# A gated product split whole instead of in four blocks, and three scalings queued behind the gate's splits, in a two-layer decoder trunk

## The chip, the cores and the metric

The kernel runs on one core of one Trainium2 chip. The metric is device time of one execution in microseconds (us), the median of several executions. Engine names are those of the profile: PE (matrix multiply), PEld (its weight loads), DVE (vector), ACT (activation), POOL (GpSimd), SP (the queue that issues most DMAs).

## What is computed

The input is one sequence of 1024 positions by 1024 channels. Layer 0 mixes positions with a chunked gating MLP, layer 1 with dilated attention, and each mixer is followed by a dense MLP. The change touches only the mixer of layer 0:

```python
def _chunk_gating_mixer(h, w_in, ln_g, ln_b, w_s, b_s, w_out):
    uv = gelu(h @ w_in)
    u, v = split(uv, 2, axis=-1)
    v = layer_norm(v, ln_g, ln_b)
    # chunks of 128 positions, 8 channel groups, causal 128x128 mixer w
    mixed = einsum('gts,bnsgc->bntgc', w, v) + b_s
    return (u * mixed) @ w_out
```

## The kernel before

Products are made of 32-bit operands split in two: `split` (L222 to L224) writes `hi`, a rounded copy, on ACT (L223) and `lo`, the rest, on DVE (L224). A product then takes three matmuls a step: weight hi with both halves of the data, weight lo with the data's hi. A weight tile needs two loads of 128x512, two copies on ACT and two subtractions on DVE.

The order of PE's instructions is the order of the text; for all other engines a list scheduler decides at build time, by priority and by when it thinks that operands are there. Once built, each engine runs its instructions in order, so one that waits holds up all behind it. `tc.issue_after(x)` puts the instructions of its block behind x on x's engine.

The work around the change, in order of time in the profile:

- **v** (up to about 130 us). x arrives in 16 tiles of 128x512 (`load_x`); `scaled(s, k)` makes the split tile `y` for half s of the positions and channel tile k (L647 on ACT, L648 on DVE) and a square of the tile for the norm (L276 on ACT, summed on POOL at L281 or on DVE at L285). In the first of three groups of chunks (`gi == 0`) the loop over k also splits the weights `w_v[k]`. At k == 7 it adds `gate_weights()` to the side work and calls `scaled(1, 0..2)` for the second half. `gate_weights` splits the causal mixer's weights into `wsh` and `wsl` (L669 to L673), multiplies them by ones and folds the sums into `rb` (L681). Then come the norm's root (L253), the activation of v (L729) and, for each of 8 chunks, layer norm, split and mixing (`spatial`).
- **u** (about 130 to 213 us). 16 tiles of 128x512, one for each channel tile m and half s, 24 matmuls each, in three PSUM banks `mm` in turn. The order is m = 0, 1, 2 for both halves, then 3, then 4, then 5, 6, 7, in each case half 0 before half 1. `u_out` empties a bank: scaling by the norm (L784, DVE, high priority; it sets the bank free), Gelu (L785, ACT), and four products of 128x128 with the mixed v (L788, DVE), written into the four `vg` tiles of the half. `u_split(s)`, called after the last tile of half s, splits the products for the next matmul in 8 tiles x 4 blocks of 128x128: 32 copies on ACT and 32 subtractions on DVE.
- **w_o** (from about 214 us). Tiles in the same three banks; `add_h` (L336, DVE) empties them. The first tile reads all of half 0's split products.
- **Side work beside u and w_o**: `prepare` makes weights for the attention ahead of time. For each of six units it loads four tiles (`t<-in_w_qkv`, by SP), forms sums and differences on DVE (L527, L528, L533, L536), splits seven of them (tiles `tr`) and writes each split back by two DMAs (`wd<-tr`, L524). The four loads of the next unit are issued by SP in turn with those writes; L527 is the first that needs them (the second and third).

Of the kernel before, what the change touches and what calls it, by code (L numbers as in the profile page):

```python
# [12 lines left out]
F32 = mybir.dt.float32  # L13
F32R = mybir.dt.float32r
AF = mybir.ActivationFunctionType
ALU = mybir.AluOpType
# [15 lines left out]
def half(s):  # L32
    return slice(s * HALF, (s + 1) * HALF)


def blk(b, n=1):
    return slice(b * P, (b + n) * P)
# [89 lines left out]
def trunk(ctx: ExitStack, tc: tile.TileContext, xT, w_u, w_v, w_o, w_s, b_s, w_qkv, w_vt, w_bo, rel,  # L127
          w_up, w_dn, w_dl, vecs, onehot, outT):
    nc = tc.nc
    flow = Flow()  # L130
# [11 lines left out]
    def temp():  # L142
        return tpool.tile([P, HALF], F32, tag="t", name="t")
# [4 lines left out]
    def rtemp():  # L148
        return tpool.tile([P, HALF], F32R, tag="t", name="tr")

    def slot(shape=(P, S), dtype=F32, name="s"):

        return slots.tile(list(shape), dtype, tag="s", name=name)

    class Pair:
# [14 lines left out]
    def pair(name="y"):  # L170
        return Pair(slot((P, 2, HALF), F32R, name))
# [19 lines left out]
    def at_bank():  # L191
        return psa.tile([P, HALF], F32, tag="at", name="at")
# [27 lines left out]
        nc.tensor.matmul(idle[:, 0:P], ones, ones, start=True, stop=True)  # L220

    def split(hi, lo, src, engine=None):  # L222
        nc.scalar.activation(hi, src, AF.Copy)  # L223
        (engine or nc.vector).tensor_tensor(lo, src, hi.bitcast(F32), op=ALU.subtract)  # L224

    def weight(src, own=None):
        lo = wpool.tile([P, D], F32R, tag="w", name="wlo")
# [398 lines left out]
    vg = {}  # L626
    wsh = slot((P, 8, P), F32R, "wsh")
    wsl = slot((P, 8, P), F32R, "wsl")
# [11 lines left out]
    def scaled(s, k):  # L640

        x, g = h[k][:, half(s)], vec[:, 0, k:k + 1]
        hi, lo = pair().both()
        if (s, k) == (0, 0):
            nc.vector.tensor_scalar(hi, x, g, None, op0=ALU.mult)
        else:
            begun.append(nc.scalar.activation(hi, x, AF.Copy, scale=g).ins)  # L647
        nc.vector.scalar_tensor_tensor(lo, x, g, hi.bitcast(F32), op0=ALU.mult, op1=ALU.subtract)  # L648
        ys[s].append((hi, lo))
        sq[s].add(k)  # L650
# [3 lines left out]
        nc.scalar.activation(rsb[:, half(s)], pb, AF.Copy)  # L654
        yield 0

    gate_raw = []

    def gate_loads():
        for i in range(2):  # L660
# [5 lines left out]
    def gate_weights():  # L666

        one = rtemp()[:, 0:P]
        nc.scalar.activation(one, ones, AF.Copy)  # L669
        for i, w3 in enumerate(gate_raw):  # L670
            nc.gpsimd.affine_select(w3, w3, pattern=[[0, 4], [1, P]], compare_op=ALU.is_ge, fill=0.0,
                                    base=0, channel_multiplier=-1)
            split(wsh[:, 4 * i:4 * i + 4, :], wsl[:, 4 * i:4 * i + 4, :], w3)  # L673
        yield 6000
        for i in range(2):
            ps = at_bank()
            for e, w in enumerate((wsh, wsl)):
# [55 lines left out]
    for gi, chunks in enumerate(((0, 1, 2), (3, 4, 5), (6, 7))):  # L733
        banks = {}
        for k in range(KT):
            if gi == 0:
                load_x(0, k)
                if k >= 5:
                    load_x(1, k - 5)
            if gi == 0:  # L740
                scaled(0, k)

            with tc.issue_after(roots[0] if k == 1 else gelus[5]) if gi == 1 and k else nullcontext():
                w = weight(w_v[k])
            if gi == 0:
                if k == 5:
                    with tc.issue_after(begun[1]):
                        gate_loads()
                if k == 7:
                    flow.add(gate_weights())  # L750
                    for i in range(3):
                        scaled(1, i)
            if gi == 1:
                if k == 0:
                    flow.add(spatial())
                if k < 5:
                    load_x(1, k + 3)
                    scaled(1, k + 3)
            if k == 0:
                for i, n in enumerate(chunks):  # L760
                    for f in range(2):
                        banks[n, f] = mm_bank() if 2 * i + f >= 6 - MMB else at_bank()
            order = [(e, i, n, f) for i, n in enumerate(chunks) for f in range(2) for e in range(3)]
            if gi == 0 and k == 0:
                order.sort(key=lambda t: (t[0], t[3]))
            for e, i, n, f in order:
                x, c = ys[n // 4][k], blk(n % 4)
                matmul(banks[n, f], x[e == 1][:, c], w[e == 2][:, half(f)], start=(k == 0 and e == 0),
                       stop=(k == 7 and e == 2))
                if e == 2:  # L770
                    flow.pump()
                if k == 7 and e == 2 and f == 1:
                    if i == 0 and gi < 2:
                        for _ in sq[gi].sums():
                            pass
                        sq[gi].rms(rs[:, 4 * gi:4 * gi + 4])
                        flow.add(spread_rms(gi), 4000)
                    else:
                        v_out(banks, chunks[:i + 1])

    def u_out(m, s, ps):
        t = temp()
        with tc.high_priority(offset=PRIO):
            nc.vector.tensor_tensor(t, ps, rsb[:, half(s)], op=ALU.mult)  # L784
        nc.scalar.activation(t, t, AF.Gelu)  # L785
        for b in range(4):
            x = vg[4 * s + b][:, blk(m)]
            nc.vector.tensor_tensor(x, x, t[:, blk(b)], op=ALU.mult)  # L788

    def u_split(s):  # L790
        out = []
        for m in range(8):
            hi, lo = pair().both()
            for b in range(4):
                split(hi[:, blk(b)], lo[:, blk(b)], vg[4 * s + b][:, blk(m)])
            out.append((hi, lo))
        return out

    us = []
    for tiles in ((0, 1, 2), (3,), (4,), (5, 6, 7)):  # L800
        w = [weight(w_u[m]) for m in tiles]
        if tiles[0] == 3:
            flow.add(prepare(PREPARED[0], PACE[0]))
        for s in range(2):
            for i, m in enumerate(tiles):
                b = mm_bank()
                mm(b, w[i], KCOLS, ys[s])
                flow.until(lambda: gated[4 * s + 3].t is not None)
                u_out(m, s, b)
            if tiles[-1] == 7:  # L810
                us.append(u_split(s))


    sq = [Square(half(0)), Square(half(1))]
# [814 lines left out]
    whole = {}  # L1629
# [316 lines left out]
```

## Time and profile before

| | us |
|---|---|
| median of 3 runs | 2121.05 (2119.27 to 2121.4) |
| profiled execution | 2123.05 |
| its span on the core | 2121.3 |
| PE busy | 2096.6 (99%) |
| DVE busy | 1580.1 (74%) |
| ACT busy | 1183.2 (56%) |
| POOL busy | 497.2 (23%) |

The profiled execution took 2123.05 us, of which 2121.3 us are the span that the profile shows; 1.75 us lie around it. PE is busy almost throughout, so time can be lost or won only where PE pauses. The views that matter are the list of what PE waited for, the time line of the engine that it waited for there, and the granted clock in stretches.

### The profile page before, as it was taken

Reading aid. Unit: us, or ns where it says so; the run is one execution under the profiler, and the core shown is the slowest. Engines: PE = TensorE matmul, PEld = TensorE weight load, DVE = VectorE, ACT = ScalarE, POOL = GpSimd, SP = SyncE. Lnnn points to the kernel's source line nnn. Section 1 sums busy time; section 2 is a strip of 40 time slices with the busy share of each in tenths; the row PEclk is TensorE's granted clock in tenths of the full one; section 3 lists DMA queues with packets and bytes.
Section 4 is the critical chain, followed back from the end, with each engine's and each line's share of the span. In section 5 each row is a group of like instructions: output and inputs, shape, how many; then the busy total and the mean of one; then the engine's idle time right before and its main releaser. Section 6 shows DMA issues by size and latency. Waiting matters only on the chain.

```text
span 2121.3 us, 30732 instructions
## 1 busy us (share of the span) xinstructions
PE 2096.6 (99%) x10160; PEld 1734.1 (82%) x10160; DVE 1580.1 (74%) x2902; ACT 1183.2 (56%) x2387; POOL 497.2 (23%) x368
## 2 busy tenths in 40 slices
PE   9999999999999999999999999999999999999998
PEld 7888788888888888778888888888888888888887
DVE  7877859766689998888746666766985446987776
ACT  7645536566665555345556665766555556544432
POOL 2000114333223233430000000002442232433244
PEclk9999999999999999999999999999999999999999
DMA  6328913678765767643865656582256443655432
GB/s 219 117 86 287 320 45 121 206 271 271 258 222 192 233 215 224 229 163 147 309 205 149 183 157 175 166 279 70 75 199 204 159 150 128 205 164 160 143 114 80
DMA packets 224756, 387.10 MB, mean 182 GB/s; under 512 B 39897, under 2 KB 67668, under 8 KB 224596
## 3 DMA queue, kind: packets, MB, share of 16 engines
q1 hardware_dynamic: 215456, 383.77, 55.0%
q10 hardware_dynamic: 9140, 1.36, 0.4%
q8 instruction: 80, 1.31, 0.3%
q14 instruction: 80, 0.66, 0.1%
HBM read 252.24 MB, written 132.81 MB: 182 GB/s over the span
## 4 chain that ended last, share of the span: by engine, by line
PE 89%; DVE 5%; DMA 2%; ACT 1%; issue 1%; POOL 1%; SPq 0%; DVEq 0%; POOLq 0%; ACTq 0%
PE mm L195 46%; PE at L195 41%; PE at L202 2%; DMA h<-in_xT 1%; DVE y L224 1%; DVE t L224 1%; DVE wp L224 0%; DVE r L441 0%; DMA r<-in_w_vt 0%; DVE hx L224 0%; DVE b L446 0%; DMA r<-in_w_dn 0%; DVE t L1867 0%; DVE h L336 0%; DVE h L1074 0%
## 5 line engine op out<-in xcount | busy, mean ns | idle before, releaser
L224 DVE TENSOR_TENSOR wp<-r,wp 128x512 fp32r<-128x512 f32 (+3 forms) x399 | 325.0, 820 | 123.0 <-ACT wp L223 120.7
L223 ACT ACTIVATE wp<-r 128x512 fp32r<-128x512 f32 (+3 forms) x399 | 235.9, 596 | 314.1 <-PE at L195 194.7
L195 PE MATMUL mm<-t,wp 128*128 128x512 f32 x1368 | 345.2, 396 | 0.6 <-DVE t L996 0.6
L195 PE MATMUL at<-hx,wp 128*128 128x512 f32 x1452 | 341.1, 389 | 1.7 <-DVE h L1074 1.7
L195 PEld LDWEIGHTS at<-hx,wp 128*128 128x128 f32 x1452 | 272.1, 188 | 60.0 <-DVE h L1074 3.3
L195 PEld LDWEIGHTS mm<-t,wp 128*128 128x128 f32 x1368 | 250.6, 188 | 53.4 <-DVE t L996 1.0
L281 POOL TENSOR_TENSOR t<-t 128x512 f32<-128x512 f32 (+1 forms) x60 | 77.4, 1291 | 814.3 <-ACT t L276 647.3
L195 PE MATMUL at<-y,wp 128*128 128x512 f32 x1008 | 245.3, 389 | 0.0
L195 PE MATMUL mm<-hx,wp 128*128 128x512 f32 x984 | 234.2, 389 | 0.7 <-ACT mm L1097 0.7
L195 PEld LDWEIGHTS at<-y,wp 128*128 128x128 f32 x1008 | 189.0, 188 | 39.6 <-issue 0.4
L195 PEld LDWEIGHTS mm<-hx,wp 128*128 128x128 f32 x984 | 184.6, 188 | 39.4 <-ACT mm L1097 1.1
L195 PE MATMUL mm<-y,wp 128*128 128x512 f32 x816 | 210.2, 397 | 1.1 <-DVE y L224 0.6
L379 POOL TENSOR_TENSOR t<-r 128x512 f32<-128x512 f32 (+3 forms) x62 | 83.2, 1342 | 478.3 <-DMA r<-in_w_up 142.2
L195 PEld LDWEIGHTS mm<-y,wp 128*128 128x128 f32 x816 | 149.1, 188 | 33.0 <-DVE y L224 1.0
L224 DVE TENSOR_TENSOR hx<-t,hx 128x512 fp32r<-128x512 f32 x192 | 159.8, 837 | 5.8 <-ACT hx L223 5.7
L195 PE MATMUL mm<-y,whi 128*128 128x512 f32 x512 | 158.4, 390 | 2.0 <-DVE t L784 2.0
L223 ACT ACTIVATE hx<-t 128x512 fp32r<-128x512 f32 x192 | 118.7, 627 | 24.5 <-DMA t<-hid 16.0
L195 PE MATMUL at<-t,wp 128*128 128x512 f32 x552 | 130.6, 389 | 0.0
L381 POOL TENSOR_TENSOR r<-r 128x512 f32<-128x512 f32 (+3 forms) x62 | 90.8, 1465 | 165.8 <-DVE wp L224 148.6
L195 PEld LDWEIGHTS at<-t,wp 128*128 128x128 f32 x552 | 103.6, 188 | 21.5
L1074 DVE TENSOR_TENSOR h<-h,at 128x512 f32<-128x512 f32 x144 | 97.8, 680 | 27.3 <-PE at L195 26.8
L195 PEld LDWEIGHTS mm<-y,whi 128*128 128x128 f32 x512 | 95.5, 188 | 21.9 <-issue 2.4
(247 smaller groups left out, 3498.3 us busy)
## 6 DMA issues: line engine op xcount, KB each, us to landing
t<-hid SPq DMA_DIRECT2D x182, 256.0 KB, 4.1
wd<-tr SPq DMA_DIRECT2D x154, 256.0 KB, 3.2
wp<-wd SPq DMA_DIRECT2D x77, 512.0 KB, 4.2
hid<-t SPq DMA_DIRECT2D x140, 256.0 KB, 2.9
r<-in_w_up SPq DMA_DIRECT2D x120, 256.0 KB, 2.9
r<-in_w_dn SPq DMA_DIRECT2D x80, 256.0 KB, 2.7
hid<-b SPq DMA_DIRECT2D x56, 256.0 KB, 2.8
r<-in_w_v SPq DMA_DIRECT2D x48, 256.0 KB, 3.1
```

The lines of the kernel that those rows point to most:

```text
L195: nc.tensor.matmul(out, lhsT, rhs, **kw)
L202: nc.tensor.transpose(out, src, ident)
L223: nc.scalar.activation(hi, src, AF.Copy)
L224: (engine or nc.vector).tensor_tensor(lo, src, hi.bitcast(F32), op=ALU.subtract)
L281: nc.gpsimd.tensor_tensor(self.acc, self.acc, sq, op=ALU.add)
L379: tt(r3, r[0, 0], r[1, 0], op=ALU.subtract)
L381: tt(r[1, 1], r[1, 0], r[0, 0], op=ALU.subtract)
L1074: return engine.tensor_tensor(hs[i, s], hs[i, s], src, op=ALU.add).ins
```

## The change

In `u_out` 11 of the 16 tiles (all 8 of half 0, and m = 5, 6, 7 of half 1) write the four products into u's own tile `t` instead of into `vg`, and split it at once as one tile of 128x512. The other five (m = 0 to 4 of half 1) are made as before and split in blocks, now right after m = 7 of half 0 instead of at the end of half 1. In the first group of v the side work `gate_weights` is begun before the three scalings, and these stand behind the last gate split on both ACT and DVE.

```diff
     def split(hi, lo, src, engine=None):
-        nc.scalar.activation(hi, src, AF.Copy)
-        (engine or nc.vector).tensor_tensor(lo, src, hi.bitcast(F32), op=ALU.subtract)
+        return (nc.scalar.activation(hi, src, AF.Copy).ins,
+                (engine or nc.vector).tensor_tensor(lo, src, hi.bitcast(F32), op=ALU.subtract).ins)
...
-            split(wsh[:, 4 * i:4 * i + 4, :], wsl[:, 4 * i:4 * i + 4, :], w3)
+            gate_split[:] = split(wsh[:, 4 * i:4 * i + 4, :], wsl[:, 4 * i:4 * i + 4, :], w3)
...
                 if k == 7:
-                    flow.add(gate_weights())
-                    for i in range(3):
-                        scaled(1, i)
+                    gate = gate_weights()
+                    flow.add(gate, next(gate))
+                    with tc.issue_after(gate_split[0]), tc.issue_after(gate_split[1]):
+                        for i in range(3):
+                            scaled(1, i)
...
-    def u_out(m, s, ps):
+    us = [[None] * 8 for _ in range(2)]
+
+    def u_out(m, s, ps, whole):
         t = temp()
         with tc.high_priority(offset=PRIO):
             nc.vector.tensor_tensor(t, ps, rsb[:, half(s)], op=ALU.mult)
         nc.scalar.activation(t, t, AF.Gelu)
         for b in range(4):
             x = vg[4 * s + b][:, blk(m)]
-            nc.vector.tensor_tensor(x, x, t[:, blk(b)], op=ALU.mult)
-
-    def u_split(s):
-        out = []
-        for m in range(8):
-            hi, lo = pair().both()
-            for b in range(4):
-                split(hi[:, blk(b)], lo[:, blk(b)], vg[4 * s + b][:, blk(m)])
-            out.append((hi, lo))
-        return out
+            nc.vector.tensor_tensor(t[:, blk(b)] if whole else x, x, t[:, blk(b)], op=ALU.mult)
+        if whole:
+            x = pair().split(t)
+            us[s][m] = x.hi, x.lo
+
+    def u_split(s, m):
+        hi, lo = pair().both()
+        for b in range(4):
+            split(hi[:, blk(b)], lo[:, blk(b)], vg[4 * s + b][:, blk(m)])
+        us[s][m] = hi, lo
...
-                u_out(m, s, b)
-            if tiles[-1] == 7:
-                us.append(u_split(s))
+                u_out(m, s, b, s == 0 or tiles[-1] == 7)
+            if tiles[-1] == 7 and s == 0:
+                for m in range(tiles[0]):
+                    u_split(1, m)
```

Because a scheduler orders ACT, DVE and SP, three places show what became of this. On PE the instructions are the same ones; only the four products with the gate's weights and a transpose stand a few places earlier. Tile names: `y` is a split tile for a matmul, `t` a temporary, `tr` a split of the side work, `wlo` the rest of a weight, `vg` the gated v. In the changed kernel L784 is L788 and L788 is L792.

ACT at the end of the first group of v, before:

```order
L276 ACTIVATE t<-h 128x512
L647 ACTIVATE y<-h,vec 128x512
L276 ACTIVATE t<-h 128x512
L669 ACTIVATE tr<-ones 128x128
L223 ACTIVATE wsh<-b 128x512 x2
L223 ACTIVATE whi<-r 128x512 x2
L276 ACTIVATE t<-h 128x512
L253 ACT_TABLE_LOAD
```

and now:

```order
L276 ACTIVATE t<-h 128x512
L669 ACTIVATE tr<-ones 128x128
L223 ACTIVATE wsh<-b 128x512 x2
L647 ACTIVATE y<-h,vec 128x512
L276 ACTIVATE t<-h 128x512
L647 ACTIVATE y<-h,vec 128x512
L276 ACTIVATE t<-h 128x512
L647 ACTIVATE y<-h,vec 128x512
L276 ACTIVATE t<-h 128x512
L223 ACTIVATE whi<-r 128x512 x2
L276 ACTIVATE t<-h 128x512
L253 ACT_TABLE_LOAD
```

The copies of the gate's weights moved ahead of the three scalings and their squares; everything from `whi` on stands where it stood, behind the same instructions.

DVE from the scaling of u's tile m = 7, half 0, to that of m = 5, half 1, before:

```order
L784 TENSOR_TENSOR t<-mm,rsb 128x512
L536 TENSOR_TENSOR t<-t 128x512
L224 TENSOR_TENSOR y<-vg,y 128x128
L788 TENSOR_TENSOR vg<-vg,t 128x128 x4
L224 TENSOR_TENSOR y<-vg,y 128x128 x12
L224 TENSOR_TENSOR tr<-t,tr 128x512
L224 TENSOR_TENSOR y<-vg,y 128x128 x2
L224 TENSOR_TENSOR tr<-t,tr 128x512
L224 TENSOR_TENSOR y<-vg,y 128x128 x18
L224 TENSOR_TENSOR wlo<-r,whi 128x512 x2
L224 TENSOR_TENSOR tr<-t,tr 128x512
L784 TENSOR_TENSOR t<-mm,rsb 128x512
```

and now:

```order
L788 TENSOR_TENSOR t<-mm,rsb 128x512
L533 TENSOR_TENSOR t<-t 128x512
L536 TENSOR_TENSOR t<-t 128x512
L792 TENSOR_TENSOR t<-vg,t 128x128 x4
L224 TENSOR_TENSOR tr<-t,tr 128x512
L224 TENSOR_TENSOR wlo<-r,whi 128x512
L224 TENSOR_TENSOR y<-t,y 128x512
L224 TENSOR_TENSOR y<-vg,y 128x128 x20
L224 TENSOR_TENSOR tr<-t,tr 128x512
L224 TENSOR_TENSOR wlo<-r,whi 128x512 x3
L224 TENSOR_TENSOR tr<-t,tr 128x512
L788 TENSOR_TENSOR t<-mm,rsb 128x512
```

Of 33 block splits 20 are left between the two scalings, the five tiles of half 1 that are still made in blocks; one whole split, two splits of weights and one combination of the side work came in. The last `tr` but one (`tr` of unit 3, number 3) stood ahead of 18 of the block splits and stands now behind all 20.

DVE from that scaling (m = 5, half 1) to the next one (m = 6), before:

```order
L784 TENSOR_TENSOR t<-mm,rsb 128x512
L224 TENSOR_TENSOR tr<-t,tr 128x512
L527 TENSOR_TENSOR t<-t 128x512
L788 TENSOR_TENSOR vg<-vg,t 128x128 x4
L528 TENSOR_TENSOR t<-t 128x512
L224 TENSOR_TENSOR y<-vg,y 128x128 x4
L224 TENSOR_TENSOR tr<-t,tr 128x512
L784 TENSOR_TENSOR t<-mm,rsb 128x512
```

and now:

```order
L788 TENSOR_TENSOR t<-mm,rsb 128x512
L527 TENSOR_TENSOR t<-t 128x512
L224 TENSOR_TENSOR tr<-t,tr 128x512
L792 TENSOR_TENSOR t<-vg,t 128x128 x4
L528 TENSOR_TENSOR t<-t 128x512
L224 TENSOR_TENSOR wlo<-r,whi 128x512
L224 TENSOR_TENSOR y<-t,y 128x512
L224 TENSOR_TENSOR tr<-t,tr 128x512
L788 TENSOR_TENSOR t<-mm,rsb 128x512
```

L527, the first to need the next unit's loads, moved from second to first place behind the scaling, and a split of weights came in.

SP where the loads of the next unit stand, before:

```order
L524 DMA wd_7_149<-tr 128x512
L184 DMA r<-in_w_o 128x512
L524 DMA wd_7_149<-tr 128x512
L524 DMA wd_3_152<-tr 128x512 x2
L184 DMA t<-in_w_qkv 128x512 x4
L524 DMA wd_4_153<-tr 128x512 x2
```

and now:

```order
L524 DMA wd_7_149<-tr 128x512 x2
L184 DMA r<-in_w_o 128x512
L524 DMA wd_3_152<-tr 128x512
L184 DMA t<-in_w_qkv 128x512
L524 DMA wd_3_152<-tr 128x512
L184 DMA t<-in_w_qkv 128x512 x3
L524 DMA wd_4_153<-tr 128x512 x2
```

Three of the four loads still stand behind the write of that `tr`, number 3 (`wd_3`); one load went ahead of it.

More of the change, by code (lines that the diff above doesn't have):

```diff
@@ L655, in spread_rms @@
         yield 0
-    gate_raw = []
+    gate_raw, gate_split = [], []
     def gate_loads():
@@ L787, in u_out @@
             x = vg[4 * s + b][:, blk(m)]
-            nc.vector.tensor_tensor(x, x, t[:, blk(b)], op=ALU.mult)
-    def u_split(s):
-        out = []
-        for m in range(8):
-            hi, lo = pair().both()
-            for b in range(4):
-                split(hi[:, blk(b)], lo[:, blk(b)], vg[4 * s + b][:, blk(m)])
-            out.append((hi, lo))
-        return out
-    us = []
+            nc.vector.tensor_tensor(t[:, blk(b)] if whole else x, x, t[:, blk(b)], op=ALU.mult)
[7 more added lines that the diff above has]
+        us[s][m] = hi, lo
     for tiles in ((0, 1, 2), (3,), (4,), (5, 6, 7)):
```

## The prediction

> **What bounds the kernel now.** First the page: PE is busy 99% of the span.
>
> ```profile
> PE 2096.6 (99%) x10160; PEld 1734.1 (82%) x10160; DVE 1580.1 (74%) x2902; ACT 1183.2 (56%) x2387; POOL 497.2 (23%) x368
> ```
>
> The change takes no instruction from PE. So it can gain only what PE waits in the stages of v, u and w_o, and lose only by a new wait. The list of what PE waited for, asked for the first 100 us and for 100 to 345 us, holds three waits worth the name (line, releaser, us in total, times, longest):
>
> ```profile
> PE at L195 <- DVE wlo L224: 2.3, 1, 2.3
> PE at L195 <- ACT vg L729: 1.0, 1, 1.0
> PE mm L195 <- DVE t L784: 2.0, 1, 2.0
> ```
>
> PE's time line places them (start, duration, what, idle before it):
>
> ```profile
> 43.19 0.50 PE L195 MATMUL at<-wlo,y 128*128 128x512 f32 x1 [2.28 <-DVE wlo L224]
> 45.79 1.22 PE L195 MATMUL at<-whi,y 128*128 128x512 f32 x2 [0.97 <-ACT vg L729]
> 215.89 0.70 PE L195 MATMUL mm<-y,whi 128*128 128x512 f32 x2 [1.98 <-DVE t L784]
> ```
>
> Two pauses stand at the end of the first group of v, one at the first tile of w_o. Between and after them, up to 345 us, PE streams, and all that ACT and DVE do there is hidden. The chain of waits gives PE's pace: 213 matmuls in 48.41 us, 0.227 us each, so a tile of 24 takes 5.45 us.
>
> ```profile
> 148.53 48.41 PE mm L195 x213
> ```
>
> **The change, part by part.**
>
> *Whole splits.* DVE's time line around the third pause:
>
> ```profile
> 203.32 0.69 DVE L784 TENSOR_TENSOR t<-mm,rsb 128x512 f32<-128x512 f32 x1
> 205.58 2.51 DVE L224 TENSOR_TENSOR y<-vg,y 128x128 fp32r<-128x128 f32 x12
> 209.01 0.69 DVE L224 TENSOR_TENSOR tr<-t,tr 128x512 fp32r<-128x512 f32 x1
> 209.61 3.73 DVE L224 TENSOR_TENSOR y<-vg,y 128x128 fp32r<-128x128 f32 x18
> 213.24 1.31 DVE L224 TENSOR_TENSOR wlo<-r,whi 128x512 fp32r<-128x512 f32 x2
> 214.44 0.70 DVE L224 TENSOR_TENSOR tr<-t,tr 128x512 fp32r<-128x512 f32 x1
> 215.04 0.70 DVE L784 TENSOR_TENSOR t<-mm,rsb 128x512 f32<-128x512 f32 x1
> 215.64 0.70 DVE L224 TENSOR_TENSOR tr<-t,tr 128x512 fp32r<-128x512 f32 x1
> 216.24 0.70 DVE L527 TENSOR_TENSOR t<-t 128x512 f32<-128x512 f32 x1
> 216.84 0.91 DVE L788 TENSOR_TENSOR vg<-vg,t 128x128 f32<-128x128 f32 x4
> 217.65 0.71 DVE L528 TENSOR_TENSOR t<-t 128x512 f32<-128x512 f32 x1
> 219.67 0.70 DVE L784 TENSOR_TENSOR t<-mm,rsb 128x512 f32<-128x512 f32 x1
> ```
>
> From start to start a whole tile costs 0.60 us (214.44, 215.04, 215.64), a block split (213.24 - 209.61) / 18 = 0.202, the four products 217.65 - 216.84 = 0.81. So a whole split saves DVE 4 x 0.202 - 0.60 = 0.21 us, 11 of them 2.3 us. None of that lies on the path but what stands ahead of the scalings L784, since these free the banks.
>
> *The third pause.* PE's tiles take three banks in turn, so the first tile of w_o needs the bank of u's m = 5, half 1. That tile was done two tiles before 213.9, where PE stopped, but its scaling stood at 215.04, behind a burst of block splits. PE resumed 0.85 us after that start. The time from the scaling of m = 7, half 0, to it was 215.04 - 203.32 = 11.72 us without a gap. The order of the changed kernel has between the same two: the scaling itself, two combinations, three `tr`, four weight splits, one whole split, so 1 + 2 + 3 + 4 + 1 = 11 steps of 0.60, four products, 20 block splits: 6.60 + 0.81 + 4.04 = 11.45. Gained: 0.27. What left the burst was largely filled up by whole-tile work. Against it, the first scaling may itself start late by a split that stands ahead of it, 0 to 0.60. I take 0 for the sum of the two; the ends are -0.3 and +0.3, a pause of 1.7 to 2.3.
>
> *A fourth pause.* Behind the scaling of m = 5 now stands L527 directly, and it needs the second and third load of the next unit. The chain of waits shows how these went before:
>
> ```profile
> 209.73 0.32 SPq L524
> 210.10 0.44 SPq L184
> 210.59 0.47 SPq L184
> 211.10 4.04 DMA t<-in_w_qkv
> ```
>
> SP issues the write of `tr` number 3 at 209.73, as soon as its split ends (209.01 + 0.69); then come the loads, each about 0.5 later. The third, at 211.10, is the one that L527 needs last. From issue to landing the four took
>
> ```profile
> DMA to landing us min/median/max: 3.1/3.9/4.6
> ```
>
> and since the four go out together, the third is more like the upper half: I take 4.3, with ends of 3.1 and 4.6. So it landed at about 215.4, and L527 at 216.24 did not wait.
>
> Now that split stands behind all 20 block splits. Counted back from the scaling at 215.04: one `tr` 0.60, three weight splits 1.80, the split itself 0.60: it starts at 212.04 and ends at 212.73. Before it ended at 209.70, so the write is 3.0 us later. Behind it one load fewer stands before the one that matters, so the third load is issued at 211.10 + 3.03 - 0.5 = 213.6 and lands at 217.9 (216.7 to 218.2). L527's turn comes at 215.64: DVE waits 2.3 us (1.1 to 2.6), with the scaling of m = 6 queued behind. From L527 to that scaling the new order has six whole steps (L527, `tr`, L528, a weight split, a whole split, `tr`) and four products: 6 x 0.60 + 0.81 = 4.41. It starts at 217.9 + 4.4 = 222.3, and PE can resume 0.85 later, at 223.2.
>
> PE wants that bank for its second tile of w_o at 215.89 + 5.45 = 221.34. Before the scaling stood at 219.67, 0.8 us ahead of need by the same 0.85. Now a pause of 1.8 us arises, 0.6 with the lower landing and 2.1 with the upper. The bank after it: from the scaling of m = 6 to that of m = 7 the new order has eight whole steps (that scaling, `tr`, a weight split, L533, `tr`, a whole split, L536, `tr`) and four products, 4.80 + 0.81 = 5.61, against PE's 5.45: 0.2 more. Together +2.0 us (+0.6 to +2.3).
>
> *The scalings behind the gate's splits.* ACT's time line:
>
> ```profile
> 33.67 0.72 ACT L647 ACTIVATE y<-h,vec 128x512 fp32r<-128x512 f32 x1 [3.78 <-DMA h<-in_xT]
> 38.42 1.14 ACT L223 ACTIVATE wsh<-b 128x512 fp32r<-128x512 f32 x2
> 39.47 1.14 ACT L223 ACTIVATE whi<-r 128x512 fp32r<-128x512 f32 x2
> 43.76 1.28 ACT L729 ACT_TABLE_LOAD   x1
> 45.05 1.85 ACT L729 ACTIVATE vg<-at,rs 128x512 f32<-128x512 f32 x3
> ```
>
> ACT starts at 33.67, when a tile of x lands, and runs to 45.05 without an idle note between. The changed order has the same instructions in this stretch; `whi` stays behind the same sum. So `whi` ends when it did and L729 stands where it did. On DVE, `wsl` took
>
> ```profile
> 39.08 2.38 DVE L224 TENSOR_TENSOR wsl<-b,wsh 128x512 fp32r<-128x512 f32 x2
> 41.38 2.35 DVE L224 TENSOR_TENSOR wlo<-r,whi 128x512 fp32r<-128x512 f32 x2
> ```
>
> and moves up with ACT's copies. From 33.67 to 38.42 ACT runs four pairs of scaling and square, less than 1.2 us each; three of them now come after the copies, so `wsl` is earlier by some 3.4 us, and `wlo` can follow `whi` from 40.0 instead of 41.38. That shortens the first pause by up to 1.4 us. But its three or four matmuls then wait for the bank that L729 frees at 45.05 all the same: what the first pause loses the second gains. PE goes on at 45.79 as before. Value 0; ends: -1.4 if that bank were not the limit, +1.0 if the gate's products, now ahead of the transpose, wait once as long as the 0.97 above.
>
> Nothing else moves on PE. u's tile `t` is held some 2 us longer, until its split; the loads on SP stand behind writes, not behind it, so I cost that at 0, and at the +0.5 of one DMA issue if it delays one.
>
> **The sum.** 0 + 2.0 + 0 = +2.0 us on a span of 2121.3, so 2123.3; with the 1.75 us around it the profiled execution would take 2125.05 instead of 2123.05. The profiled execution lies 2.0 us above the median of the runs, so the median becomes 2121.05 + 2.0 = 2123.05. A difference of 0.2% (4.2 us) is about what a measurement of this kernel can tell from no change, and this is half of that.
>
> **Rivals.** *The clock falls* (slower). PE's granted clock in stretches (start:end, then busy us of PE, PEld, DVE, ACT, POOL, then the clock):
>
> ```profile
> 41.49:44.90 3.41, 1.46 (x4) 0.67 (x4) 3.34 (x9) 3.38 (x5) 1.09 (x1) 1.00 0.14 41
> 44.90:48.31 3.41, 2.52 (x8) 2.12 (x9) 3.21 (x9) 3.40 (x7) 0.00 (x0) 0.50 0.83 265
> 48.31:51.73 3.42, 3.42 (x9) 2.65 (x9) 1.92 (x7) 3.39 (x6) 0.00 (x0) 0.50 0.00 1
> 212.15:215.57 3.42, 1.77 (x8) 1.13 (x6) 3.42 (x10) 1.67 (x3) 0.00 (x0) 1.00 1.02 313
> 215.57:218.98 3.41, 3.09 (x14) 2.60 (x15) 3.41 (x12) 2.14 (x7) 0.00 (x0) 1.00 0.97 326
> ```
>
> After a stretch of 3.41 us with PE busy for 1.46 the clock was 0.50 for two such stretches; after one with 1.77 it stayed at 1.00. The third pause is close to that edge: at 2.3 us instead of 1.98, or with the stretches cut otherwise, PE is busy for as little as 3.41 - 2.3 = 1.1. Then one to two stretches run at half clock, a loss of 1.7 to 3.4 us. With the fourth pause of 2.0 behind it that is 2123.05 + 1.7 to 3.4, 2124.8 to 2126.5; I take 2126, slower by 0.23%. It decides from a pause of 3.41 - 1.77 = 1.6 to 3.41 - 1.46 = 2.0 us within one stretch. For it: two pauses within 10 us. Against: a slow tile of w_o gives DVE time to catch up, so the fourth pause shrinks.
>
> [...]
>
> *The loads come in time.* With landings as short as 3.1 us and the burst shorter by its 0.27, the fourth pause is 0.6 and the third 1.7: 2121.05 + 0.6 - 0.3 = 2121.35, no change. For it: the row's lower end. Against: the third of four loads that share the queues.
>
> *Faster.* The third pause goes (-2.0), and a first stage with another spread of its pauses keeps the clock at 1.00: the 5.9 us from 45.79 to 51.73 ran at 0.50 and lost half, 3.0. Together 2116.0, faster by 0.24%. Against it: DVE gains 0.27 us where 2.0 are needed, and the six matmuls that come earlier fall into the same stretch.
>
> **Chances.** The two pauses without the clock, 2123: 0.40. The clock falls, 2126: 0.35. The loads come in time, 2121.35: 0.15. Faster, 2116: 0.10. So slower by over 0.2% has 0.35, within 0.2% 0.55, faster 0.10. The range goes from 2119.3 (the third pause gains its 0.3 and the first its 1.4: 2121.05 - 1.7) to 2127.1 (third pause +0.3, upper landing +2.3, two stretches at half clock +3.4: 2121.05 + 6.0), which leaves out the faster case and little above.
>
> **What would show it.** PE's list should have L788 twice, near 213.9 and near 221.3, the second 1 to 2 us; DVE's time line an idle note before L527 that names the loads; the pauses of v should sum to about 3.4 us as before and end at 45.8. A clock of 0.50 near 216 to 223 would be the first rival. The forecast is wrong if L527 does not wait, or if the scaling of m = 5 comes before 214.

## The result, and the profile after

The changed kernel takes 2125.2 us in the median of 13 runs (2123.07 to 2129.56), the kernel before 2120.21 us in 13 runs (2119.27 to 2123.08): a ratio of 1.0024, with a 95% interval of 1.0017 to 1.0032. It is 5.0 us slower. The forecast was 2123.05, +2.0.

The two profiled executions would have said "no change": 2123.05 us before and 2123.07 after. The first is one of the slowest of its kernel, the second the fastest of its own. So the stages are compared, not the spans. The same two instructions in both, the first scaling of u on DVE and the root of the norm behind w_o on ACT; before:

```profile
125.68 0.69 DVE L784 TENSOR_TENSOR t<-mm,rsb 128x512 f32<-128x512 f32 x1
...
285.65 0.26 ACT L253 ACTIVATE sd<-at,scalars 128x4 f32<-128x4 f32 x1 [1.53 <-PE at L195]
```

and after:

```profile
123.58 0.68 DVE L788 TENSOR_TENSOR t<-mm,rsb 128x512 f32<-128x512 f32 x1
...
287.14 0.26 ACT L253 ACTIVATE sd<-at,scalars 128x4 f32<-128x4 f32 x1 [1.53 <-PE at L195]
```

The stage between them, u and w_o, grew from 159.97 to 163.56 us, by 3.6. Ahead of it the profiled execution of before was 2.1 us later (its clock was 0.50 from 44.90 to 51.73, as the prediction shows, where after had 1.00), and behind it the one of after was 1.5 faster (2123.05 - 285.65 = 1837.4 against 2123.07 - 287.14 = 1835.9). Those two hide the 3.6.

What PE waited for after, in the first 100 us and from 100 to 345 us (us in total, times, longest):

```profile
PE at L195 <- DVE rv L255: 1.2, 1, 1.2
...
PE at L195 <- ACT vg L729: 0.9, 1, 0.9
PE at L195 <- ACT y L647: 0.6, 1, 0.6
PE at L195 <- DVE rb L681: 0.5, 1, 0.5
...
PE mm L195 <- DVE t L788: 5.1, 2, 3.4
```

In v the two pauses of before (2.3 and 1.0) are cut into smaller ones; the four rows shown and two smaller ones of 0.3 and 0.2 sum to 3.7, against 3.5 before (2.3, 1.0 and one of 0.2). At w_o there are two waits on the scaling where there was one. PE's time line has the end of the pauses in v, and the two ahead of the first and the second tile of w_o:

```profile
45.69 0.73 PE L195 MATMUL at<-whi,y 128*128 128x512 f32 x2 [0.91 <-ACT vg L729]
...
213.50 0.70 PE L195 MATMUL mm<-y,whi 128*128 128x512 f32 x2 [1.71 <-DVE t L788]
...
222.60 0.74 PE L195 MATMUL mm<-y,whi 128*128 128x512 f32 x2 [3.37 <-DVE t L788]
```

DVE's time line has the scaling of m = 7, half 0 (201.20), the split of `tr` number 3 behind the burst (209.65), the scalings of m = 5 (212.66) and m = 6 (221.86), and L527 between them, which waited 4.08 us for its loads and held up what stands behind it on DVE, the scaling of m = 6 among it:

```profile
201.20 0.68 DVE L788 TENSOR_TENSOR t<-mm,rsb 128x512 f32<-128x512 f32 x1
...
209.65 0.70 DVE L224 TENSOR_TENSOR tr<-t,tr 128x512 fp32r<-128x512 f32 x1
...
212.66 0.70 DVE L788 TENSOR_TENSOR t<-mm,rsb 128x512 f32<-128x512 f32 x1
217.43 0.69 DVE L527 TENSOR_TENSOR t<-t 128x512 f32<-128x512 f32 x1 [4.08 <-DMA t<-in_w_qkv]
...
221.86 0.69 DVE L788 TENSOR_TENSOR t<-mm,rsb 128x512 f32<-128x512 f32 x1
```

SP issued the loads where the order said, one between the two writes of that `tr` and three behind them:

```profile
209.18 0.32 SPq L524 DMA_DIRECT2D wd<-tr  x1
209.55 0.42 SPq L184 DMA_DIRECT2D t<-in_w_qkv  x1
210.37 0.32 SPq L524 DMA_DIRECT2D wd<-tr  x1
210.74 1.46 SPq L184 DMA_DIRECT2D t<-in_w_qkv  x3
```

But the third load, the one that L527 needs last, landed 6.1 us after its issue. Before, the slowest landing that the profile shows took 4.6. It shows two of the four: the first and the fourth before, the first (2.9) and the third (6.1) after.

```profile
DMA to landing us min/median/max: 2.9/4.5/6.1
```

### The profile page after: what moved, and what is told of

Its sections match the earlier page's. It is cut to its first block, busy times and chain, and to the rows that moved or that the text cites. A ratio compares the mean times of both kernels' runs of the same rounds, so it can differ in the third digit from the quotient of the medians.

```text
span 2121.3 us, 30670 instructions
## 1 busy us (share of the span) xinstructions
PE 2094.1 (99%) x10160; PEld 1731.6 (82%) x10160; DVE 1576.6 (74%) x2869; ACT 1180.9 (56%) x2354; POOL 494.1 (23%) x368
## 4 chain that ended last, share of the span: by engine, by line
PE 87%; DVE 7%; DMA 3%; ACT 2%; issue 1%; POOL 1%; SPq 0%; DVEq 0%; POOLq 0%; ACTq 0%
PE mm L195 44%; PE at L195 41%; PE at L202 2%; DVE y L224 1%; DVE t L224 1%; DMA r<-in_w_v 1%; DVE tr L224 0%; DVE hx L224 0%; DVE r L441 0%; DVE wp L224 0%; DMA t<-hid_(0, 0)_6161 0%; DVE b L446 0%; DMA h<-in_xT 0%; DVE h L1078 0%; DVE wlo L224 0%
```

## The experiments

Theory A: the loss is L527's wait on late loads, behind a burst that has used up the time by which the three banks let PE run ahead, and some of it a lower clock behind the pauses (before, 0.50 was granted from 44.90, 1.7 us behind the end of the pause of 2.28). The rivals are named with each run. Line numbers shift by up to five in the edited kernels; the scaling that frees u's banks is L784 to L789. In the table the last column is the length of the stage of u and w_o in the profiled execution, between the two instructions used above (before 159.97, after 163.56).

| run | us, median (runs) | before, same chip | ratio, 95% | stage |
|---|---|---|---|---|
| whole splits alone | 2125.56 (11) | 2121.32 | 1.0014 to 1.0031 | 165.01 |
| scalings alone | 2120.2 (11) | 2121.32 | 0.9986 to 1.0004 | 158.36 |
| after, loads one step earlier | 2119.38 (11) | 2121.32 | 0.9984 to 1.0001 | 156.21 |
| after, PE filled in both pauses | 2125.71 (9) | 2121.32 | 1.0012 to 1.0032 | 162.16 |
| after, block splits last | 2125.9 (8) | 2119.58 | 1.0019 to 1.0039 | 164.25 |
| before, loads one step earlier | 2127.95 (5) | 2119.58 | 1.0022 to 1.0048 | 167.36 |
| after, PE filled in the second pause | 2125.68 (11) | 2119.58 | 1.0018 to 1.0036 | 163.02 |
| after, second profile | 2126.01 (11) | 2119.58 | 1.0019 to 1.0037 | 162.80 |
| after, loads behind both writes | 2123.39 (11) | 2119.74 | 1.0009 to 1.0027 | 162.81 |
| before, loads two steps earlier | 2130.45 (5) | 2119.74 | 1.0037 to 1.0062 | 169.15 |
| before, second profile | 2120.59 (8) | 2119.74 | 0.9992 to 1.0012 | 158.76 |
| after, loads one step earlier, second profile | 2119.29 (11) | 2119.74 | 0.9989 to 1.0007 | 157.34 |

### The two parts alone

The whole splits alone: the changed kernel with the first group of v as before.

```diff
-                    gate = gate_weights()
-                    flow.add(gate, next(gate))
-                    with tc.issue_after(gate_split[0]), tc.issue_after(gate_split[1]):
-                        for i in range(3):
-                            scaled(1, i)
+                    flow.add(gate_weights())
+                    for i in range(3):
+                        scaled(1, i)
```

> The whole-tile splits alone; the scalings stay ahead of the gate's splits. Order of DVE and SP at the start of w_o is that of the changed kernel. Theory A (the whole difference is the wait of L527 on late loads at the start of w_o, plus the lower clock that its pause brings): two waits on L788, 1.7 and 2 to 3.5 us, near 214 and 221; first pauses 2.3 and 1.0 as before; time 2123 to 2126, 3 to 6 above the kernel before. Theory B (the scalings behind the gate's splits cost as well): no more than 2 above the kernel before, the rest is in the next run.

The scalings alone: the kernel before with that edit the other way round.

> The scalings behind the gate's splits alone; u is split in blocks as before. Theory A: one wait on DVE at the start of w_o, 2.0 us; the pauses at the end of the first group of v sum to 3.3 as before, cut in other pieces; time within 1 us of the kernel before, 2119.5 to 2121. Theory B: 2 to 3 us above the kernel before.

Measured: the splits alone bring the whole loss, 2125.56, 4.2 us above the kernel before; the scalings alone give 2120.2, no difference that can be told. In the profile of the splits alone L527 waits 4.45 us. The first pauses, expected at 2.3 and 1.0, were 1.3 and 0.9; the second wait on the scaling, expected at 2 to 3.5, was 3.78. PE's second pause at w_o, and the granted clock behind it (start:end, then busy us of PE, PEld, DVE, ACT, POOL, then clock, DMA share, GB/s):

```profile
224.52 0.99 PE L195 MATMUL mm<-y,whi 128*128 128x512 f32 x2 [3.78 <-DVE t L786]
```

```profile
221.41:224.82 3.41, 0.30 (x1) 0.30 (x2) 3.41 (x7) 3.05 (x6) 0.00 (x0) 1.00 0.79 244
224.82:228.23 3.41, 3.41 (x9) 2.63 (x8) 3.41 (x10) 1.46 (x3) 0.00 (x0) 0.50 1.03 348
```

The second pause is followed by one stretch at half clock, in which nine matmuls stand where 3.41 / 0.227 = 15 fit at full clock. With the scalings alone one wait is left at w_o, 1.1 us where 2.0 was expected (the two profiles of before have 2.0 and 1.4):

```profile
PE mm L195 <- DVE t L786: 1.1, 1, 1.1
```

So the loss is the first part's: theory A's time came, and theory B falls.

### The loads one step earlier

```diff
-                if p == 4 and i != unit_list[-1]:
+                if p == 3 and i != unit_list[-1]:
                     coming = raws(unit_list[m + 1])
```

> The changed kernel with the next unit's four loads issued one split of the side work earlier, ahead of the write of tr number 3. Theory A: L527 does not wait, the second wait on L788 is gone. Between the scalings of m = 7, half 0, and m = 5, half 1, stand 8 whole steps, four products and 20 block splits, 4.8 + 0.8 + 4.0 = 9.6 us instead of 11.5, so the first wait on L788 falls from 1.7 to 0 to 0.5 as well. Time 2118 to 2120, at or below the kernel before. Theory C (the pauses come from the amount of DVE work, not from the loads): still 2 us or more of waits on L788 and 2122 or more.

Measured: 2119.38, and 2119.29 when it was measured again (below). The longest of PE's waits from 100 to 345 us is now another:

```profile
PE mm L195 <- ACT t L847: 0.4, 1, 0.4
```

Both waits on L788 are gone. L527 runs ahead of the scaling without a wait, and that scaling comes 9.91 us (209.22 - 199.31) behind the one of m = 7, against 11.46 after (9.6 were expected):

```profile
199.31 0.69 DVE L788 TENSOR_TENSOR t<-mm,rsb 128x512 f32<-128x512 f32 x1
...
208.02 0.69 DVE L527 TENSOR_TENSOR t<-t 128x512 f32<-128x512 f32 x1
...
209.22 0.69 DVE L788 TENSOR_TENSOR t<-mm,rsb 128x512 f32<-128x512 f32 x1
```

Moving four loads undoes the loss of 4 to 6 us. The burst of 20 block splits is still there, but the edit also took 1.55 us of other DVE work out from between the two scalings (11.46 to 9.91), which accounts for most of the first wait (1.7 and 2.1 us in the two profiles of the changed kernel). The second wait, up to 3.4 us, went with the wait of L527: from the scaling of m = 5 to that of m = 6 it was 9.20 us (221.86 - 212.66), 4.08 of them that wait, and is 5.02 now (from 209.22 to 214.24). So theory A holds for the second wait, and theory C (the amount of DVE work) falls for it.

### Is it the wait that costs, or the clock?

Two kernels fill PE's pauses with products whose results go unused (the second kernel ahead of the second tile alone; each product shows as two instructions in the time line), and the changed kernel was profiled once more.

```diff
+    fill = at_bank()
     for tiles in ((0, 1), (2,), (3,), (4, 5, 6, 7)):
...
             for i, m in enumerate(tiles):
+                if s == 0 and m < 2:
+                    for _ in range((6, 10)[m]):
+                        nc.tensor.matmul(fill[:, 0:P], ones, ones, start=True, stop=True)
                 b = mm_bank()
```

> The changed kernel with 6 and 10 products of ones by ones (128x128, 0.22 us each, results unused) on PE ahead of the first and the second tile of w_o, that is inside the two pauses, so that PE is never idle long enough there for its clock to fall. Theory A: the pauses are still there (less the 1.3 and 2.2 us that the filling takes of them), the granted clock is 0.997 or more in all runs, and the time falls from about 2125 to 2123 to 2123.5, close to the fastest run of the changed kernel. Theory D (the clock has no part; the executions above 2124 are slow for another reason, such as transfers): 2125 as the changed kernel.

> The changed kernel with ten products of ones by ones ahead of the second tile of w_o alone, inside the longer pause. Theory A (clock): clock 0.997 or more in nearly all runs; the time of runs whose later load of w_vt at 905 us is not late falls to 2123 to 2124. Theory D (the clock has little part, executions differ by when loads land): median 2125 again although the clock is up.

> The changed kernel once more, for a second profile of it and its runs beside the others on one chip. Theory A: median 2124.5 to 2126; L527 waits 3.5 to 5 us again, two waits on L788 of 1.7 and 3 to 4 us; if the profiled execution is above 2124.5, its granted clock shows 0.5 in one or two stretches of 3.4 us, at 45 to 52 or behind 221. Theory D: no stretch at 0.5, a longer wait of L527 or a wait elsewhere instead.

Measured: the products took 0.25 us each ahead of the first tile (1.50 / 6) and 0.24 ahead of the second (2.39 / 10), where 0.22 was expected. With both pauses filled, the granted clock was 0.997 or 0.998 in all 9 runs (0.995 to 0.998 in those of the changed kernel), and yet the median is 2125.71. PE's time line shows the filling where it was meant to be, with what is left of the waits behind it:

```profile
211.15 1.50 PE L827 MATMUL at<-ones 128*128 128x128 f32 x12
212.82 0.70 PE L195 MATMUL mm<-y,whi 128*128 128x512 f32 x2 [0.16 <-DVE t L788]
...
218.35 2.39 PE L827 MATMUL at<-ones 128*128 128x128 f32 x20
221.65 0.74 PE L195 MATMUL mm<-y,whi 128*128 128x512 f32 x2 [0.91 <-DVE t L788]
```

PE gets to the second tile hardly sooner than without the filling: 221.65 - 212.82 = 8.8 us behind the first, against 9.1 after. The second profile of the changed kernel shows why a lower clock need not cost anything here. Its pauses, and its clock:

```profile
213.61 0.71 PE L195 MATMUL mm<-y,whi 128*128 128x512 f32 x2 [2.05 <-DVE t L788]
...
222.59 0.73 PE L195 MATMUL mm<-y,whi 128*128 128x512 f32 x2 [1.69 <-DVE t L788]
```

```profile
210.76:214.17 3.41, 1.36 (x7) 0.84 (x6) 2.70 (x5) 2.45 (x5) 0.00 (x0) 1.00 0.90 223
214.17:217.59 3.42, 3.42 (x10) 2.65 (x9) 0.17 (x1) 0.02 (x1) 0.00 (x0) 0.50 1.00 319
```

The first tile of w_o ran 3.4 us of its time at half clock, and the pause behind it shrank from 3.37 to 1.69; the second tile starts at 222.59 where it started at 222.60. L527, behind its loads, stands at 217.42 there (217.43 in the first profile), and the scaling behind it at 221.85 (221.86): the end is set by the loads, through DVE. In the profile of the splits alone the half clock came behind the last pause, where no wait could take it up (from there to 345 us none of PE's is over 0.4); its stage is 165.01 long, 1.4 to 2.2 more than in the two profiles of the changed kernel, though its L527 also waited 0.4 to 0.5 longer.

So the loss is there with the clock no lower than in the kernel before (4.4 us with both pauses filled, at 0.997 or 0.998 against 0.996 to 0.998), and theory A's fall to 2123 to 2124 did not come; theory D gave the filled kernels' time. That the clock adds nothing to the changed kernel is not shown. In the 13 runs of the result the time goes with the granted clock: 2123.07 to 2123.67 in the three at 0.997 or more, 2124.77 to 2127.01 in the four at 0.996, 2125.05 to 2129.56 in the six at 0.995. Longer pauses may lie behind both; the pauses of these runs were not measured but in the profiled one. With the clock up in all runs of the filled kernel the times spread almost as wide, 2123.24 to 2129.5. In its profiled execution PE also waited 2.5 us near 905 us for another load that came late, so the medians can't say how much is the loads here and how much waits elsewhere.

### The same late loads without the burst ahead

The five block-split tiles were moved behind the products of half 1:

```diff
-            if tiles[-1] == 7 and s == 0:
+            if tiles[-1] == 7 and s == 1:
                 for m in range(tiles[0]):
                     u_split(1, m)
```

> The changed kernel with the 20 block splits of half 1's five tiles moved behind the products of half 1 instead of behind m = 7 of half 0. The loads still stand behind the write of tr number 3. Between the scalings of m = 7, half 0, and m = 5, half 1, stand 10 whole steps and four products, 6.8 us instead of 11.5. Theory A (a late load costs only when the burst has already used up the slack of the three banks): L527 still waits 3 to 5 us on its loads, but the scaling of m = 6 comes in time; both waits on L788 gone or under 0.4 us; time 2118 to 2120. Theory E (a wait of L527 stalls PE by itself): a wait on L788 of 1 us or more, 2121 to 2123.

Measured: 2125.9, which neither theory gave. The mechanism came out as theory A has it, on DVE and PE:

```profile
212.47 0.69 DVE L527 TENSOR_TENSOR t<-t 128x512 f32<-128x512 f32 x1 [3.16 <-DMA t<-in_w_qkv]
...
225.97 4.12 DVE L224 TENSOR_TENSOR y<-vg,y 128x128 fp32r<-128x128 f32 x20
```

```profile
217.03 0.73 PE L195 MATMUL mm<-y,whi 128*128 128x512 f32 x2 [0.38 <-DVE t L788]
...
226.18 0.49 PE L195 MATMUL mm<-y,whi 128*128 128x512 f32 x1 [3.41 <-ACT y L223]
```

L527 waits 3.16 us and the second tile of w_o only 0.38, so a wait of L527 by itself does little; theory E falls. What I had not seen is the third tile of w_o: it is the first to read half 1's split products, and the burst stood at 225.97, behind all else, where PE waited 3.41 us for its first block. Put there, the burst stalls PE by itself.

### What makes the loads late

Over six profiles with one load between the two writes (the changed kernel twice, the splits alone, both filled kernels, the block splits last) the slowest of the four loads, as far as the profile shows their landing, took 5.8 to 6.4 us. In the two profiles with both writes ahead (before, scalings alone) it took 4.6 and 4.2. The kernel below puts all four loads behind both writes:

```diff
                 for e, t in enumerate((hi, lo)):
-                    nc.sync.dma_start(wd[i, p][:, e, :], t.bitcast(F32))
+                    put.last = nc.sync.dma_start(wd[i, p][:, e, :], t.bitcast(F32)).ins
...
-                    coming = raws(unit_list[m + 1])
+                    with tc.issue_after(put.last):
+                        coming = raws(unit_list[m + 1])
```

> The changed kernel with the next unit's four loads put behind both writes of tr number 3 on SP, where the kernel before has them, instead of one load between the two writes; DVE's order around the pauses is that of the changed kernel. Theory G (a load that is issued between the two writes makes those behind it slow: 5.8 to 6.5 us from issue to landing for the third in seven profiles of that order, 4.0 to 4.6 in three of the other): the third load is issued about 0.5 later and lands 4.0 to 4.6 later, L527 waits 2.7 to 3.3 us instead of 4.1, the pause of the second tile of w_o ends 0.8 to 1.4 earlier, time 2123.5 to 2125. Rival H (the slow loads come from the moment, when the queue fills from empty and more writes and loads follow, not from the order): again 5.8 us or more, L527 waits 4.4, time 2125.5 to 2126.5.

(The counts in that text are wrong; it was six profiles and two.) Measured: 2123.39, 3.65 above the kernel before. SP's time line, the landing, L527 and PE's second tile:

```profile
210.59 1.52 SPq L524 DMA_DIRECT2D wd<-tr  x2
212.16 1.88 SPq L184 DMA_DIRECT2D t<-in_w_qkv  x4
```

```profile
DMA to landing us min/median/max: 4.4/4.4/4.4
```

```profile
217.72 0.69 DVE L527 TENSOR_TENSOR t<-t 128x512 f32<-128x512 f32 x1 [2.95 <-DMA t<-in_w_qkv]
```

```profile
222.88 0.73 PE L195 MATMUL mm<-y,whi 128*128 128x512 f32 x2 [2.27 <-DVE t L789]
```

The one landing that the profile shows, that of the third load, is 4.4 us. L527 waits 2.95 instead of 4.08, though one load more stands between the second write and the third load, and the pause is 2.27 instead of 3.37. At this place theory G's figures came (the time a little under its 2123.5 to 2125) and rival H's did not; the second profile of before, both writes ahead, has 4.7.

As a mechanism theory G is not shown, and other loads of the same traces speak against it. In the kernel before the loads of three other units, issued from 173.04, 190.79 and 227.19, also stand four in a row behind writes, and they were about as slow as the late ones here (two or three landings each; the other two units' took up to 4.8 and 4.2):

```profile
DMA to landing us min/median/max: 4.7/5.7/6.7
DMA to landing us min/median/max: 5.7/5.8/6.0
DMA to landing us min/median/max: 2.8/5.4/5.6
```

In the two profiles of the earlier loads, all four ahead of the writes, the slowest took 4.6 and 6.0 us. And in the kernel before with the loads one step earlier (next section), where one load stands ahead of a write and three behind it, L527 waited 0.43 us for them. So 6 us is common for these loads and 4 to 5 is not tied to one order; what decides stays open.

### Do the whole splits gain anything of their own?

The kernel before, with the loads one step and two steps earlier (`p == 3`, and `p == 7` in place of `p == 4`):

> The kernel before, with the next unit's loads issued one split of the side work earlier, as in the run with earlier loads. Between the two scalings stand 5 whole steps, four products and 31 block splits, 10.1 us instead of 11.7, since fewer weights and splits of the side work fall there. Theory A: the one wait on L784 falls from 2.0 to about 0.4, time 1 to 2 us below the kernel before, 2118.5 to 2119.5, the same as the changed kernel with earlier loads: the whole-tile splits give nothing of their own. Theory F (the whole-tile splits do gain, and the loads only hid it): this stays at the time of the kernel before, 2120 to 2121.5, above the run with earlier loads.

> The kernel before, block splits and all, with the next unit's loads issued two splits of the side work earlier. Between the scalings of m = 7, half 0, and m = 5, half 1, stand 6 whole steps, four products and 20 block splits, 8.5 us; the weights of w_o's second tile stand ahead of the scaling of m = 7 and come just in time. Theory A: no wait on L784 of over 0.5 us, 2118 to 2120, at the time of the changed kernel with earlier loads, so the whole-tile splits give nothing of their own. Theory F (they do): a wait of 1 us or more is left at the start of w_o, 2120 or more.

Measured: 2127.95 and 2130.45. The first is far above the time of either theory; the second lies in theory F's open "2120 or more", but not by its wait. No wait on the scaling is left in either; instead PE waits for w_o's own weights, in the first kernel:

```profile
PE mm L195 <- ACT whi L223: 3.8, 1, 3.8
PE mm L195 <- DVE wlo L224: 2.8, 1, 2.8
```

and in the second, where SP's time line shows the reason:

```profile
253.11 1.22 PE L195 MATMUL mm<-y,whi 128*128 128x512 f32 x2 [8.47 <-ACT whi L223]
```

```profile
228.81 2.15 SPq L184 DMA_DIRECT2D t<-in_w_qkv  x4
231.07 17.90 SPq L524 DMA_DIRECT2D wd<-tr  x20
249.02 2.13 SPq L184 DMA_DIRECT2D r<-in_w_o  x4
```

The load of w_o's weights that PE waits for is issued at 249.02 at the earliest, behind four loads and 20 writes of the side work; the copy `whi` of it ran at 252.43, and PE went on at 253.11. So the same edit that removes the loss from the changed kernel adds one here, and the question stays open: theory A's "nothing of their own" was not shown.

### Second profiles

> The kernel before once more, for a second profile of its first stage. If the first stage loses to the clock in most executions of this order (a stretch at 0.5 near 45, as in the three profiles of it so far, against none there in the profiles with the scalings behind the gate's splits): 0.5 there again. If that was chance: 1.00 throughout.

> The changed kernel with the loads one step earlier, once more, against the kernel before on the same chip. Theory A: no wait on L788, 2118.5 to 2120, 0.5 to 2 us below the kernel before; if the scalings behind the gate's splits are worth nothing, the 2 us of the pause that is gone, less what the executions scatter.

The second profile of before has a clock of 1.00 from 40 to 52 us, and its first scaling of u stands at 124.17 (125.68 in the first one). With the old order of the scalings, 0.50 shows near 45 us in the first profile of before (from 44.90) and in that of the splits alone (from 43.91), not in this one; with the new order it shows in the second profile of the earlier loads (from 44.43), and the clock is 1.00 from 44 to 52 us in four: after, the scalings alone, the first profile of the earlier loads and the one with both pauses filled. That may be a small gain of the second part; the time of the scalings alone can't tell it from nothing. The earlier loads give 2119.29 against 2119.74, an interval of 0.9989 to 1.0007: the lowest median of all kernels here, 6 us under the changed kernel, and not to be told from the kernel before. The stage of u and w_o in the two profiles of this kernel is 1.4 to 3.8 us shorter than in the two of before.

## Why the prediction was right and wrong

- **The burst and the third pause: right.** 11.45 us were worked out between the two scalings, 11.46 measured (212.66 - 201.20). The pause is 1.71 and 2.05 in the two profiles; in those of before it is 1.98 and 1.38, so the 1.98 that the sum started from was the longer of two. One of the prediction's own signs of being wrong came: the scaling stands at 212.66, before 214. That is because u began 2.1 us earlier in this execution (123.58 against 125.68), and not because the burst was shorter.
- **L527 and the order behind it: right.** From L527 to the scaling of m = 6 4.41 was worked out and 4.43 measured (221.86 - 217.43); the third load is issued 1.40 ahead of the scaling of m = 5 (211.26, second of the three from 210.74, against 212.66), as worked out (213.6 against 215.04).
- **The step that failed: "I take 4.3, with ends of 3.1 and 4.6", for the landing of the third load.** It took 6.1 (issued at 211.26, L527 at 217.43). The wait of L527 became 4.08 instead of 2.3, and the fourth pause 3.37 instead of 1.8. Size, not mechanism. The range came from one row, that of this unit's loads, and the row holds two landings, the first and the fourth, not "the four". The same trace had five more such rows, with slowest landings of 6.7, 6.0 and 5.6 (shown above) and of 4.8 and 4.2: 6.1 was within what the trace of before showed. With both writes ahead the third load took 4.4, inside the ends, and the loss was 3.65 (2123.39 against 2119.74), still above the forecast of 2.0.
- **The 0.2 for the next bank** did not show: the two scalings stand 5.61 apart as worked out (227.47 behind 221.86), but PE had no further wait that the list shows.
- **The scalings at 0: right in size.** PE went on at 45.69 (45.79 before), and alone they make no difference. The reason came out otherwise: the first pause lost its time, but the second did not gain it (0.91 against 0.97); it went into new waits on `rv`, `y` and `rb` (1.2, 0.6 and 0.5).
- **The rival "The clock falls": near in time, its reason in part open.** It gave 2126, and the runs lie at 2125.2 and 2126.0. Half clock did follow the pauses in some profiles (in the second one from 214.17), but as the sentence against it said, the fourth pause shrank by what the slow tile lost (3.37 to 1.69; half of the 3.42 us at 0.50 is 1.71), and with the clock at 0.997 or 0.998 in all runs the loss was still 4.4. The pause of 1.6 to 2.0 us from which it was to decide was an estimate from two rows of before; in the runs one of 2.05 was followed by 0.50 and one of 3.37 by 1.00, so what decides was not shown. What speaks for it is that the runs of the result with the lower clock are the longer ones.
- **The rivals "The loads come in time" and "Faster" fell:** the loads came later, not sooner, and the 0.27 of DVE time did not remove the third pause.
- **The sum.** +2.0 was forecast and +5.0 measured, inside the range, but only since its upper end holds 3.4 us for two stretches at half clock; without them it would end at 2123.65. With the clock's part open, that it lies inside is in part luck. Of the three outcomes the one given most, within 0.2% (0.55), did not come; slower by over 0.2% had 0.35. The stage of u and w_o grew by 3.8 us in the mean of two profiles each (163.56 and 162.80 against 159.97 and 158.76). Over all profiles of the two orders (the changed kernel twice, the splits alone and the two filled kernels; before twice and the scalings alone) it is 163.3 against 159.0, 4.3 us. The medians differ by 5.0 (interval 3.6 to 6.8) and 6.4 (4.0 to 7.8). What lies between is not settled; what follows w_o took 1835.9 and 1838.3 us in two executions of the changed kernel and 1837.4 and 1836.7 before, a scatter with no side, in which PE's wait on L1101 near 900 us, again behind a load, is 0.4 in one execution and 1.6 in the other.

## What to carry to other kernels

Where DVE or ACT runs side work in a queue with the work that frees PE's banks, look first at the DMA that the side work waits for, and at what that DMA stands behind on its own queue: four loads issued one step earlier were worth the whole loss here, though the same edit cost the kernel before 8 us, where w_o's weights then came late. A landing time read from one group of loads is one sample: look at the same loads elsewhere in the trace before giving a range (4.6 here, up to 6.7 for the other units). And compare stage by stage, since two executions of one kernel may differ by more than the change.

## What the hardware showed unexpectedly

The loads that were slow ran while the DMA rate was low. In the same stretch of 3.4 us, before:

```profile
211.80:215.20 3.40, 2.12 (x10) 1.42 (x8) 3.40 (x12) 2.02 (x4) 0.00 (x0) 1.00 1.00 299
```

and after:

```profile
211.80:215.20 3.40, 1.70 (x7) 1.43 (x8) 1.55 (x3) 1.70 (x3) 0.00 (x0) 1.00 0.77 169
```

299 GB/s against 169, though the loads and writes had been issued. It does not take the new order: in the kernel before, while the loads issued from 190.79 were under way (5.7 to 6.0 us), the rate was as low:

```profile
192.30:195.70 3.40, 3.40 (x17) 2.81 (x16) 0.91 (x3) 0.00 (x0) 0.00 (x0) 1.00 0.61 148
```

So slow landings and a low rate go together in these stretches; why was not found.

The clock did not follow the length of the pause alone. A pause of 3.37 us was followed by a clock of 1.00 in one execution of the changed kernel (220.80 to 224.21), one of 2.05 by 0.50 in the other (214.17 to 217.59). In the stretches read here the half clock lasted 3.41 us (from 224.82 with the splits alone), 3.42 (from 214.17 in the second profile of the changed kernel) or 6.83 (44.90 to 51.73 in before, 43.91 to 50.74 with the splits alone). It began 0.30 us behind the end of a pause with the splits alone (224.52), 0.56 in the second profile of the changed kernel (213.61) and 1.71 in before (43.19). What decides whether a pause is followed by it was not found.
